# RWKV heads on their own row halves instead of a block-diagonal state, in a hybrid recurrent layer

## The chip, the cores and the metric

The kernel runs on one core of a Trainium2 chip. TensorE (PE) multiplies, VectorE (DVE), ScalarE (ACT) and GpSimd (POOL) do the elementwise work, and SyncE (SP), ACT and POOL issue the DMAs. The metric is the device time of one execution in microseconds (us); lower is better.

## The reference

One layer of a decoder trunk, for a prompt of 1024 tokens and for 8 single-token sequences that continue from given states:

```python
xn = _rmsnorm(x, norm1_g)
P  = xn @ w_in                       # one projection, its columns split among three groups
o_r, S_r = _rwkv7(...)               # 6 heads x 64: generalised delta rule
o_h, S_h = _hgrn2(...)               # 6 heads x 64: gated linear attention in chunks of 64
o_l, ... = _rglru(...)               # 256 channels: gated linear recurrence
x = x + concat(o_r, o_h, o_l) @ w_out
x = x + square(relu(_rmsnorm(x, norm2_g) @ w1)) @ w2      # 1024 -> 4096 -> 1024
y = _rmsnorm(x, final_g)
```

The change lies in the first group. For each head and token, with a 64x64 state S (value x key):

```python
sa = S @ (-kk_t)
S  = S * w_t + outer(sa, kk_t * a_t) + outer(v_t, k_t)
o  = S @ r_t
```

All arithmetic is fp32. Outputs are y for both groups and all final states.

## The kernel before

The kernel has two stages. In the first (to about 870 us) the input projection, the three recurrent groups and the output projection are woven together; in the second the MLP runs as dense matmuls. Dense products are three fp32r matmuls of 128x128 weights each (high and low parts), so the weights arrive twice: once through SP, once as an accumulating DMA that POOL issues (L267). Everything else on TensorE is plain fp32, where a matmul is two instructions in the trace.

**Order of the work.** Only TensorE's order is written by hand. `weave` (L82) is a planner: each piece of work is a generator that issues instructions and then yields either a delay in us or the name of an event it waits for. The planner keeps a clock `now`, which `mm` (L70) and `tr` (L75) advance by an estimated cost (0.08 for a 64x64x64 fp32 matmul, 0.11 for a transpose), and takes the stream that is ready; where none is, it issues dense matmuls of the projection as filler. Delays are the constants D1 to D42. The other engines' order follows from priorities. A late operand therefore stops TensorE and all that is queued behind it.

**RWKV.** Two heads share a tile of 128 channels, so there are 3 pairs j, and each half of the prompt (hf) is cut into two quarters of 256 tokens: 12 parts q (`PARTS`), each of NQ = 4 chunks of C = 64 tokens. Four generators work on each part:

- `rw_operands` (L490) makes decays and keys. It transposes v into `uv` (vT, L536 to L541: 2 transposes of 128x128, 2 ACT copies), writes the key operands `kb` (L544, L548) and `ar` (L549, L550), and transposes `kb` into `kbt` (L555 to L559: 4 transposes of 128x128, one ACT copy).
- `rw_inverse` (L573) runs as two streams, one for the even and one for the odd parts. It makes the scores `sc` (L583 to L592): for each head 4 matmuls of 64 rows by 128 columns, then a mask on DVE, with the delay D10 between the heads. Then it inverts unit triangular 64x64 blocks in five doublings (W and Y), and forms mv (L643).
- `rw_chain` (L651) goes through the chunks in order. For each: `ar` times the state (L667) and an add (rh, L669); ym times rh (L674) and a copy into uv (L675); then kbt times uv (L679), the output products with the state (L682) and with sc (L685), the decayed state on POOL (L690) and the new state (L696).
- `rw_finish` (L712) normalises, transposes the output back (oT, L730 to L732) and applies the gate.

The state of a pair is block-diagonal, 128x128, with zeros off the blocks; one matmul of 128 contracted rows serves both heads. A chunk's solved values lie on one half of the rows, by the parity of the chunk (`brow[c % 2]`), for both heads; `units` (L484) goes through the heads outside and the chunks inside.

**PSUM.** The banks have tags: `ra` (2 banks) for sc, W, Y and mv of both inverse streams, `ch` (1) for the chain, `o` (1) for the small products of operands, finish and the gated recurrence, `h` (2) and `big` (2) for the rest. A tile of a tag waits until the one that had its bank has been read.

Of the kernel before, what the change touches and what calls it, by code (L numbers as in the profile page):

```python
# [17 lines left out]
P = 128  # L18
D = 1024
# [31 lines left out]
def kernel(ctx: ExitStack, tc: tile.TileContext, i, o):  # L51
# [432 lines left out]
    def units():  # L484

        for h in range(2):
            for c in range(NQ):
                yield c, h, brow[c % 2], slice(((c // 2) * 2 + h) * C, ((c // 2) * 2 + h) * C + C)

    def rw_operands(q):  # L490
# [38 lines left out]
        kb = rwp.tile([P, NQ // 2, 4, C], F32, tag="kb", name=f"kb_{n}", bufs=1)  # L529
# [12 lines left out]
        ck4 = "p (c x t) -> p c x t"  # L542
        V.scalar_tensor_tensor(t5, t3, 1.0, t4, op0=ALU.add, op1=ALU.mult)
        V.scalar_tensor_tensor(kb[:, :, 1:3, :], t5.rearrange(ck4, x=2, t=C), 0.5, t1.rearrange(ck4, x=2, t=C),  # L544
                               op0=ALU.mult, op1=ALU.mult)
        V.tensor_scalar(t3, t3, hka[:, j:j + 1], omka[:, j:j + 1], op0=ALU.mult, op1=ALU.add)
        V.tensor_tensor(t3, t3, k_, op=ALU.mult)
        V.tensor_tensor(kb[:, :, 0:4:3, :], t3.rearrange(ck4, x=2, t=C), t1.rearrange(ck4, x=2, t=C), op=ALU.mult)  # L548
# [10 lines left out]
        S.copy(kbt, pt.rearrange("p (c x) -> p c x", x=P))  # L559
# [13 lines left out]
    def rw_inverse(q):  # L573
# [9 lines left out]
        for h in range(2):  # L583
            hp = slice(h * 64, h * 64 + 64)
            pt = ps("ra", f"sc{h}_{n}")
            for c in range(NQ):
                mm(pt[:, c * P:(c + 1) * P],
                   kb[hp, c // 2, 2 * (c % 2):2 * (c % 2) + 2, :].rearrange("p x t -> p (x t)"),
                   ar[hp, c, :, :].rearrange("p x t -> p (x t)"))
            V.tensor_tensor(sc.rearrange("p (c h) x -> p h c x", h=2)[:, h], pt.rearrange("p (c x) -> p c x", x=P),  # L590
                            bc(smask.rearrange("p x t -> p (x t)")[:, None, :], [P, NQ, P]), op=ALU.mult)
            if h == 0:  # L592
                yield D10
        ev(("sc", q), 0.0)
        sc5 = sc.rearrange("p (c e h) x -> p c e h x", e=2, h=2)
        for e in range(2):
            V.copy_predicated(ym[brow[e]].rearrange("p (c h) t -> p c h t", h=2),
                              bc(lmask[brow[e], 0, None, None, :].bitcast(I32), [64, NQ // 2, 2, 64]),
                              sc5[brow[e], :, e, :, 0:64])
# [44 lines left out]
        for c, h, b, cc in units():  # L644
            mm(pt[b, cc], sc[krow[c % 2], 2 * c + h, 0:64], uv[krow[c % 2], c, h * 64:h * 64 + 64])
# [5 lines left out]
    def rw_chain(q):  # L651
# [5 lines left out]
        pt = ps("ch", f"ch_{n}")  # L657
        po = pt[:, QT:2 * QT]
        for c in range(NQ):
            st = rw_state[j]  # L660
            b = brow[c % 2]
            first = st is None
            mv = xm[b, (c // 2) * 2:(c // 2) * 2 + 2, :].rearrange("p h v -> p (h v)")
            if first:
                rh = mv
            else:
                mm(pt[b, 0:P], ar[:, c, 0, :], st)  # L667
                rht = rwp.tile([P, P], F32, tag="rh", name=f"rh{c}_{n}", bufs=1)
                V.tensor_tensor(rht[b, :], pt[b, 0:P], mv, op=ALU.add)  # L669
                rh = rht[b, :]  # L670
# [4 lines left out]
            V.tensor_copy(uv[b, c, :], pt[b, 0:P])  # L675
# [12 lines left out]
            if not first:  # L688
                ws = rwp.tile([P, P], F32, tag="ws", name=f"ws{c}_{n}", bufs=2)
                G.tensor_scalar(ws, st, wc, 0.0, op0=ALU.mult, op1=ALU.add)  # L690
# [21 lines left out]
    def rw_finish(q):  # L712
# [18 lines left out]
        for c in range(NQ // 2):  # L731
            tr(pt[:, c * P:(c + 1) * P], ot[:, c * P:(c + 1) * P], ident)  # L732
# [818 lines left out]
```

## Time and profile before

| | us |
|---|---|
| three runs: median (lowest to highest) | 1645.81 (1644.93 to 1648.32) |
| profiled execution: device time | 1637.81 |
| its span, first to last instruction | 1636.0 |
| TensorE busy in the span | 1536.6 |
| VectorE / ScalarE / GpSimd busy | 759.2 / 650.0 / 386.2 |
| mean granted TensorE clock | 0.962 of full |

A row of the timeline gives the start in us from the span's beginning, the time that a group of like instructions took, engine, line, operation, "out<-moving,stationary", the weights' rows*columns and the moving tile, and the count. The start of the next row minus the start of this one is the time that the group held TensorE (its "slot"); the time in the row is longer, because a matmul's end overlaps its successors. L73 is the line of `mm`, L77 that of `tr`, so TensorE's work is told apart by tile names.

### The profile page before, as it was taken

The numbers are of one execution on the slowest core, as the hardware profiler recorded it, in microseconds if no ns is written. First come the engines' busy times: TensorE is split into PE (matmuls) and PEld (weight loads), VectorE is DVE, ScalarE is ACT, GpSimd is POOL, SyncE is SP. The second block draws the span as 40 slices with busy tenths as digits, with TensorE's granted clock in tenths as the row PEclk, the third lists the DMA queues.
The fourth block names the chain that finished last, engine by engine and source line by source line (L and its number), as shares of the span: only waits on it lengthen the run. The fifth ranks groups of instructions, "written<-read, shape, count | busy, mean of one in ns | idle before, by whom it ended". The sixth has DMA issues, their size and how long they took to land.

```text
span 1636.0 us, 29373 instructions
## 1 busy us (share of the span) xinstructions
PE 1536.6 (94%) x12158; PEld 1309.2 (80%) x12158; DVE 759.2 (46%) x1752; ACT 650.0 (40%) x1374; POOL 386.2 (24%) x505
## 2 busy tenths in 40 slices
PE   6879999999899999999868899999999999999997
PEld 5657677688688788777667798989898999898887
DVE  6486656775666676675434122222222222222224
ACT  4443643644345346355434323323242323333232
POOL 3472312322323424413222111111101010111111
PEclk8989989999799999999989899999999999999999
DMA  7624424333243433335564454444445453534342
GB/s 223 149 56 101 90 65 92 78 79 85 59 93 78 105 82 91 91 85 126 137 154 109 104 103 90 98 85 101 80 99 95 90 99 83 103 78 97 59 91 104
DMA packets 56373, 159.00 MB, mean 97 GB/s; under 512 B 7312, under 2 KB 7600, under 8 KB 56240
## 3 DMA queue, kind: packets, MB, share of 16 engines
q0 software_dynamic: 26288, 77.48, 28.3%
q1 hardware_dynamic: 29808, 79.61, 14.9%
q8 instruction: 95, 1.56, 0.4%
q14 instruction: 38, 0.31, 0.1%
q10 hardware_dynamic: 144, 0.04, 0.0%
HBM read 150.93 MB, written 6.17 MB: 96 GB/s over the span
## 4 chain that ended last, share of the span: by engine, by line
PE 73%; issue 8%; DVE 7%; DMA 6%; ACT 4%; POOL 3%; POOLq 0%; ACTq 0%; DVEq 0%
PE up L73 20%; PE dn L73 18%; PE in L73 16%; PE ch L73 3%; PE out L73 3%; DMA wl_in<-in_w_in 2%; DMA wl_w<-in_w 2%; PE W L73 2%; PE Y L73 2%; DMA wl_out<-in_w_out 2%; PE sc L73 1%; PE gram L73 1%; PE ho L73 1%; DVE rq L931 1%; POOL wl_w L267 1%
## 5 line engine op out<-in xcount | busy, mean ns | idle before, releaser
L73 PE MATMUL in<-xh,wl_in 128*128 128x512 f32 (+3 forms) x648 | 224.7, 347 | 12.7 <-DMA wl_in<-in_w_in 12.7
L73 PE MATMUL in<-xl,wh_in 128*128 128x512 f32 (+3 forms) x648 | 222.9, 344 | 4.5 <-DVE xl L356 4.5
L73 PE MATMUL dn<-hh,wl_w 128*128 128x264 f32 (+2 forms) x696 | 223.3, 321 | 0.6 <-DMA wl_w<-in_w 0.6
L73 PE MATMUL in<-xh,wh_in 128*128 128x512 f32 (+3 forms) x648 | 223.4, 345 | 0.0
L73 PE MATMUL dn<-hl,wh_w 128*128 128x264 f32 (+2 forms) x696 | 222.8, 320 | 0.0
L73 PE MATMUL dn<-hh,wh_w 128*128 128x264 f32 (+2 forms) x696 | 222.6, 320 | 0.0
L267 POOL DMA_DIRECT2D wl_w<-in_w x90 | 77.3, 865 | 590.2 <-ACT hh L1369 325.7
L1439 DVE TENSOR_TENSOR mix<-mix,dn 128x512 f32<-128x512 f32 (+2 forms) x192 | 98.3, 512 | 242.4 <-PE dn L73 242.4
L262 ACT ACTIVATE wh_w<-raw_w 128x512 fp32r<-128x512 f32 (+1 forms) x90 | 70.6, 785 | 275.1 <-PE dn L73 225.3
L1368 DVE SCALAR_TENSOR_TENSOR rl<-up,rl 128x512 f32<-128x512 f32 (+2 forms) x96 | 49.5, 516 | 219.1 <-ACT rl L1367 219.1
L73 PEld LDWEIGHTS in<-xh,wl_in 128*128 128x128 f32 x648 | 126.9, 196 | 29.4 <-DMA wl_in<-in_w_in 15.1
L73 PE MATMUL up<-nxh,wh_w 128*128 128x264 f32 (+1 forms) x512 | 144.9, 283 | 1.4 <-DVE rl L1368 1.3
L73 PE MATMUL up<-nxl,wh_w 128*128 128x264 f32 (+1 forms) x512 | 144.1, 281 | 0.5 <-POOL nxl L1267 0.5
L73 PE MATMUL up<-nxh,wl_w 128*128 128x264 f32 (+1 forms) x512 | 144.4, 282 | 0.0
L73 PEld LDWEIGHTS dn<-hh,wl_w 128*128 128x128 f32 x696 | 130.8, 188 | 14.3 <-DMA wl_w<-in_w 4.6
L73 PEld LDWEIGHTS in<-xl,wh_in 128*128 128x128 f32 x648 | 126.7, 195 | 17.9 <-DVE xl L356 4.8
L73 PEld LDWEIGHTS in<-xh,wh_in 128*128 128x128 f32 x648 | 126.8, 196 | 15.7 <-issue 4.7
L73 PEld LDWEIGHTS dn<-hl,wh_w 128*128 128x128 f32 x696 | 130.9, 188 | 10.1
L73 PEld LDWEIGHTS dn<-hh,wh_w 128*128 128x128 f32 x696 | 131.0, 188 | 9.4
L73 PE MATMUL up<-nh,wl_w 128*128 128x512 f32 x256 | 102.8, 402 | 8.4 <-DMA wl_w<-in_w 8.4
L1367 ACT ACTIVATE rl<-up 128x512 f32<-128x512 f32 (+2 forms) x96 | 43.3, 451 | 152.7 <-PE up L73 152.7
L73 PE MATMUL up<-nh,wh_w 128*128 128x512 f32 x256 | 102.5, 400 | 0.0
(436 smaller groups left out, 3228.6 us busy)
## 6 DMA issues: line engine op xcount, KB each, us to landing
raw_in<-in_w_in SPq DMA_DIRECT2D x53, 512.0 KB, 3.4
wl_in<-in_w_in POOLq DMA_DIRECT2D x52, 512.0 KB, 5.5
raw_w<-in_w SPq DMA_DIRECT2D x32, 512.0 KB, 3.3
wl_w<-in_w POOLq DMA_DIRECT2D x32, 512.0 KB, 5.5
raw_w<-in_w SPq DMA_DIRECT2D x64, 256.0 KB, 2.7
wl_w<-in_w POOLq DMA_DIRECT2D x58, 256.0 KB, 4.1
raw_out<-in_w_out SPq DMA_DIRECT2D x16, 512.0 KB, 3.4
wl_out<-in_w_out POOLq DMA_DIRECT2D x16, 512.0 KB, 5.5
```

Of the source, the lines that this page charges most:

```text
L73: PE.matmul(out, lhsT, rhs, start=start, stop=stop)
L262: act(wh[:, ks], raw[:, ks], AF.Copy)
L267: G.dma_start(wl[:, ks], src[:, ks], accum_op=ALU.add)
L931: V.tensor_tensor(rq[hp, h, :].rearrange("p (m j) -> p m j", j=hh), k4[hp, :, 1, :], q4[hp, :, 1, :], op=ALU.mult)
L1367: act(rl[:, :n], pt[:, :n], AF.Relu)
L1368: V.scalar_tensor_tensor(rl[:, :n], pt[:, :n], 0.0, rl[:, :n], op0=ALU.max, op1=ALU.mult)
L1439: V.tensor_tensor(x2[m][:, c0:c0 + n], x2[m][:, c0:c0 + n], pt[:, :n], op=ALU.add)
```

## The change

Head h of a pair is put on its own half of the rows throughout. The state becomes 128x64 and is no longer cleared at the start; products with it are two matmuls of 64x64 instead of one with 128 contracted rows. `units` goes through the chunks outside and the heads inside, so successive matmuls lie on alternating halves. vT and oT become 8 matmuls of 64x64 with an identity instead of 2 transposes of 128x128; kbt becomes 8 transposes of 64x128 in two groups with a delay D4 between them; kb holds three blocks per chunk, one of which ACT copies. The scores of both heads go to both `ra` banks at once, halves alternating, without the delay D10. In the chain uv is copied in two instructions instead of one and the state updated in one instead of two. The state written out is 128x64 instead of 128x128.

```diff
-    rw_st = [[rwp.tile([P, P], F32, name=f"st{j}_{q}") for q in range(2)] for j in range(3)]
-    for st in rw_st:
-        for q in range(2):
-            G.memset(st[q], 0.0)
-    brow = (slice(64, 128), slice(0, 64))
-    krow = (slice(0, 64), slice(64, 128))
+    rw_st = [[rwp.tile([P, C], F32, name=f"st{j}_{q}") for q in range(2)] for j in range(3)]
+
+    brow = (slice(0, 64), slice(64, 128))
+    krow = (slice(64, 128), slice(0, 64))
...
-        for h in range(2):
-            for c in range(NQ):
-                yield c, h, brow[c % 2], slice(((c // 2) * 2 + h) * C, ((c // 2) * 2 + h) * C + C)
+        for c in range(NQ):
+            for h in range(2):
+                yield c, h, brow[h], slice(c * C, c * C + C)
...
-        pt = ps("o", f"vT_{n}")
-        for c in range(NQ // 2):
-            tr(pt[:, c * P:(c + 1) * P], v[:, q0 + c * P:q0 + (c + 1) * P], ident)
-        pt4 = pt[:, 0:NQ // 2 * P].rearrange("p (c x) -> p c x", x=P)
-        S.copy(uv[0:64, 0:NQ:2, :], pt4[0:64])
-        S.copy(uv[64:128, 1:NQ:2, :], pt4[64:128])
+        pt = ps("o", f"vT_{n}")[:, 0:QT]
+        for c, h, b, cc in units():
+            mm(pt[krow[h], cc], v[b, q0 + c * C:q0 + c * C + C], ident[b, b])
+        for h in range(2):
+            S.copy(uv[krow[h], :, h * 64:h * 64 + 64], ck(pt[krow[h]]))
...
+        S.copy(kb[:, :, 2, :], kb[:, :, 0, :])
...
-        pt = ps("o", f"kbt_{n}")
-        for c in range(NQ):
-            src = kb[:, c // 2, 2 * (c % 2):2 * (c % 2) + 2, :].rearrange("p x t -> p (x t)")
-            tr(pt[:, c * P:(c + 1) * P], src, ident)
-        S.copy(kbt, pt.rearrange("p (c x) -> p c x", x=P))
+        for h in range(2):
+            b = brow[h]
+            pt = ps("o", f"kbt{h}_{n}")[:, 0:QT]
+            for c in range(NQ):
+                tr(pt[:, c * C:c * C + C], kb[b, c, h:h + 2, :].rearrange("p x t -> p (x t)"), ident[b, b])
+            S.copy(kbt[:, :, b], ck(pt))
+            if h == 0:
+                yield D4
...
-        for h in range(2):
-            hp = slice(h * 64, h * 64 + 64)
-            pt = ps("ra", f"sc{h}_{n}")
-            for c in range(NQ):
-                mm(pt[:, c * P:(c + 1) * P],
-                   kb[hp, c // 2, 2 * (c % 2):2 * (c % 2) + 2, :].rearrange("p x t -> p (x t)"),
-                   ar[hp, c, :, :].rearrange("p x t -> p (x t)"))
...
-            if h == 0:
-                yield D10
+        pts = [ps("ra", f"sc{h}_{n}") for h in range(2)]
+        for c, h, b, _ in units():
+            mm(pts[h][:, c * P:(c + 1) * P], kb[b, c, h:h + 2, :].rearrange("p x t -> p (x t)"),
+               ar[b, c, :, :].rearrange("p x t -> p (x t)"))
...
-                mm(pt[b, 0:P], ar[:, c, 0, :], st)
-                rht = rwp.tile([P, P], F32, tag="rh", name=f"rh{c}_{n}", bufs=1)
-                V.tensor_tensor(rht[b, :], pt[b, 0:P], mv, op=ALU.add)
+                for b in brow:
+                    mm(pa[b], ar[b, c, 0, :], st[b])
+                rht = rwp.tile([P, C], F32, tag="rh", name=f"rh{c}_{n}", bufs=1)
+                V.tensor_tensor(rht, pa, rh, op=ALU.add)
...
-            for h in range(2):
-                hc = slice(h * 64, h * 64 + 64)
-                mm(pt[b, hc], ym[b, (c // 2) * 2 + h, :], rh[:, hc])
-            V.tensor_copy(uv[b, c, :], pt[b, 0:P])
+            for b in brow:
+                mm(pu[b], ym[b, c, :], rh[b])
+            for b in brow:
+                V.tensor_copy(uv[b, c, b], pu[b])
             yield D17
-            for h in range(2):
-                hp = slice(h * 64, h * 64 + 64)
-                mm(pt[hp, P:P + 64], kbt[:, c, hp], uv[:, c, hp])
-            out = po[krow[c % 2], (c // 2) * P:(c // 2) * P + P]
+            for b in brow:
+                mm(pst[b], kbt[:, c, b], uv[:, c, b])
+            out = po[:, c * C:c * C + C]
             if not first:
-                mm(out, ar[:, c, 1, :], st, stop=False)
-            for h in range(2):
-                hp = slice(h * 64, h * 64 + 64)
-                mm(out[:, hp], sc[:, 2 * c + h, 64:128], uv[:, c, hp], start=first, stop=first or h == 1)
+                for b in brow:
+                    mm(out[b], ar[b, c, 1, :], st[b], stop=False)
+            for h, b in enumerate(brow):
+                mm(out[b], sc[:, 2 * c + h, 64:128], uv[:, c, b], start=first, stop=True)
...
-                    V.scalar_tensor_tensor(sn[hp, hp], pt[hp, P:P + 64], wc[hp], ws[hp, hp], op0=ALU.mult, op1=ALU.add)
+                V.scalar_tensor_tensor(sn, pst, wc, ws, op0=ALU.mult, op1=ALU.add)
...
-        for c in range(NQ // 2):
-            tr(pt[:, c * P:(c + 1) * P], ot[:, c * P:(c + 1) * P], ident)
+        for c, _, b, cc in units():
+            mm(pt[b, cc], ot[b, cc], ident[b, b])
```

More of the change, by code (lines that the diff above doesn't have):

```diff
@@ L528, in rw_operands @@
         ar = rwp.tile([P, NQ, 2, C], F32, tag="ar", name=f"ar_{n}", bufs=3)
-        kb = rwp.tile([P, NQ // 2, 4, C], F32, tag="kb", name=f"kb_{n}", bufs=1)
+        kb = rwp.tile([P, NQ, 3, C], F32, tag="kb", name=f"kb_{n}", bufs=1)
         kbt = rwp.tile([P, NQ, P], F32, tag="kbt", name=f"kbt_{n}", bufs=3)
@@ L582, in rw_inverse @@
         (S.copy if q < 2 else G.tensor_copy)(ym, bc(id64[:, None, :], [P, NQ, C]))
-        for h in range(2):
-            hp = slice(h * 64, h * 64 + 64)
-            pt = ps("ra", f"sc{h}_{n}")
-            for c in range(NQ):
-                mm(pt[:, c * P:(c + 1) * P],
-                   kb[hp, c // 2, 2 * (c % 2):2 * (c % 2) + 2, :].rearrange("p x t -> p (x t)"),
-                   ar[hp, c, :, :].rearrange("p x t -> p (x t)"))
-            V.tensor_tensor(sc.rearrange("p (c h) x -> p h c x", h=2)[:, h], pt.rearrange("p (c x) -> p c x", x=P),
+        pts = [ps("ra", f"sc{h}_{n}") for h in range(2)]
[3 more added lines that the diff above has]
+        for h, b in enumerate(brow):
+            sch = sc.rearrange("p (c h) x -> p h c x", h=2)[:, h]
+            V.tensor_tensor(sch, pts[h].rearrange("p (c x) -> p c x", x=P),
                             bc(smask.rearrange("p x t -> p (x t)")[:, None, :], [P, NQ, P]), op=ALU.mult)
-            if h == 0:
-                yield D10
+            V.copy_predicated(ym[b], bc(lmask[b, 0, None, :].bitcast(I32), [64, NQ, 64]), sch[b, :, 0:64])
         ev(("sc", q), 0.0)
[L595 to L599, printed above, removed]
         ymf, xmf = (t.rearrange("p u t -> p (u t)") for t in (ym, xm))
@@ L644, in rw_inverse @@
         for c, h, b, cc in units():
-            mm(pt[b, cc], sc[krow[c % 2], 2 * c + h, 0:64], uv[krow[c % 2], c, h * 64:h * 64 + 64])
+            mm(pt[b, cc], sc[krow[h], 2 * c + h, 0:64], uv[krow[h], c, h * 64:h * 64 + 64])
         S.copy(xmf, pt)
@@ L657, in rw_chain @@
         pt = ps("ch", f"ch_{n}")
+        pa, pu, pst = (pt[:, u * C:u * C + C] for u in range(3))
         po = pt[:, QT:2 * QT]
@@ L660, in rw_chain @@
             st = rw_state[j]
-            b = brow[c % 2]
             first = st is None
[L663 to L666, printed above, removed]
-                mm(pt[b, 0:P], ar[:, c, 0, :], st)
-                rht = rwp.tile([P, P], F32, tag="rh", name=f"rh{c}_{n}", bufs=1)
-                V.tensor_tensor(rht[b, :], pt[b, 0:P], mv, op=ALU.add)
-                rh = rht[b, :]
+            rh = xm[:, c, :]
@@ L671, in rw_chain @@
+            if not first:
+                for b in brow:
+                    mm(pa[b], ar[b, c, 0, :], st[b])
+                rht = rwp.tile([P, C], F32, tag="rh", name=f"rh{c}_{n}", bufs=1)
+                V.tensor_tensor(rht, pa, rh, op=ALU.add)
+                rh = rht
                 yield D16
-            for h in range(2):
-                hc = slice(h * 64, h * 64 + 64)
-                mm(pt[b, hc], ym[b, (c // 2) * 2 + h, :], rh[:, hc])
-            V.tensor_copy(uv[b, c, :], pt[b, 0:P])
+            for b in brow:
+                mm(pu[b], ym[b, c, :], rh[b])
@@ L683, in rw_chain @@
-            for h in range(2):
-                hp = slice(h * 64, h * 64 + 64)
-                mm(out[:, hp], sc[:, 2 * c + h, 64:128], uv[:, c, hp], start=first, stop=first or h == 1)
+                for b in brow:
+                    mm(out[b], ar[b, c, 1, :], st[b], stop=False)
+            for h, b in enumerate(brow):
+                mm(out[b], sc[:, 2 * c + h, 64:128], uv[:, c, b], start=first, stop=True)
             wc = ee[:, c, C:C + 1]
             sn = rw_st[j][c % 2]
-            if not first:
-                ws = rwp.tile([P, P], F32, tag="ws", name=f"ws{c}_{n}", bufs=2)
+            if first:
+                V.tensor_scalar(sn, pst, wc, None, op0=ALU.mult)
+            else:
+                ws = rwp.tile([P, C], F32, tag="ws", name=f"ws{c}_{n}", bufs=2)
@@ L690, in rw_chain @@
                 G.tensor_scalar(ws, st, wc, 0.0, op0=ALU.mult, op1=ALU.add)
-            for h in range(2):
-                hp = slice(h * 64, h * 64 + 64)
-                if first:
-                    V.tensor_scalar(sn[hp, hp], pt[hp, P:P + 64], wc[hp], None, op0=ALU.mult)
-                else:
-                    V.scalar_tensor_tensor(sn[hp, hp], pt[hp, P:P + 64], wc[hp], ws[hp, hp], op0=ALU.mult, op1=ALU.add)
+                V.scalar_tensor_tensor(sn, pst, wc, ws, op0=ALU.mult, op1=ALU.add)
@@ L1522, in outputs @@
     sh = r["shift"].transpose(2, 1, 0).reshape(1 + NB, D)
-    wkv = r["p_wkv"].reshape(3, 2, 64, 2, 64)
-    wkv = np.stack([wkv[:, h, :, h] for h in range(2)], axis=1).reshape(1, 1, 6, 64, 64)
+    wkv = r["p_wkv"].reshape(1, 1, 6, 64, 64)
     lru = r["lru"].reshape(256, 36)
```

8 lines of the change are left out of this document (3 added, 5 removed).

## Prediction

> **What bounds the kernel now.** I read the page first, then the busy time by windows, then TensorE's waits, then its timeline around the operations that the change touches.
>
> ```profile
> span 1636.0 us, 29373 instructions
> ## 1 busy us (share of the span) xinstructions
> PE 1536.6 (94%) x12158; PEld 1309.2 (80%) x12158; DVE 759.2 (46%) x1752; ACT 650.0 (40%) x1374; POOL 386.2 (24%) x505
> ```
> ```profile
> 50.00:800.00 750.00, 705.81 (x6935) 562.43 (x6933) 484.07 (x1192) 356.90 (x863) 247.64 (x316) 0.95 0.40 91
> 800.00:870.00 70.00, 50.06 (x359) 48.83 (x360) 22.73 (x47) 24.26 (x38) 16.82 (x20) 0.85 0.54 129
> ```
> ```profile
> PE oT L77 <- DVE ot L727: 15.0, 7, 5.2
> PE out L73 <- DMA wl_out<-in_w_out: 12.5, 4, 10.4
> PE pb_kk L77 <- DVE t L247: 11.2, 4, 8.9
> PE ch L73 <- DVE rh L669: 3.3, 5, 1.7
> ```
>
> The columns of the windows are start and end, length, then busy us of PE, weight loads, DVE, ACT and POOL, the granted clock, DMA share and GB/s. All of RWKV lies in these two windows. In the 750 us from 50 to 800 TensorE is busy 706, DVE 484, ACT 357, POOL 248: TensorE is the bound, in an order that is fixed, with dense matmuls put into the gaps. It idles 44 us there. The waits that are named (times, longest last) are the output's transpose behind the normalisation, a transpose of the key norm and weights for the output projection; the chain's own wait, ch on rh, is 3.3 us. So the chain's latency is mostly covered, and what counts is how long each piece of the change holds TensorE. That is not its busy time but its slot, from its start to the next start.
>
> **The unit prices**, from the timeline at full clock.
>
> ```profile
> 759.26 0.40 PE L73 MATMUL out<-mh,wh_out 128*128 128x512 f32 x1
> 759.50 0.40 PE L73 MATMUL out<-ml,wh_out 128*128 128x512 f32 x1
> 759.83 0.43 PE L73 MATMUL ch<-st,ar 128*64 128x128 f32 x2
> 760.19 0.50 PE L73 MATMUL out<-mh,wl_out 128*128 128x512 f32 x1
> ```
> ```profile
> 762.23 0.44 PE L73 MATMUL ch<-rh,ym 64*64 64x64 f32 x4
> 762.61 0.65 PE L77 MATMUL hoT<-ident,hot 128*128 128x128 f32 x4
> 763.02 0.47 PE L73 MATMUL out<-ml,wh_out 128*128 128x512 f32 x1
> ```
> ```profile
> 764.57 0.34 PE L73 MATMUL ch<-uv,kbt 128*64 128x64 f32 x4
> 764.74 0.38 PE L73 MATMUL ch<-st,ar 128*64 128x128 f32 x2
> 764.96 0.40 PE L73 MATMUL ch<-uv,sc 128*64 128x64 f32 x4
> 765.28 0.44 PE L77 MATMUL oT<-ident,ot 128*128 128x128 f32 x2
> 765.48 0.48 PE L73 MATMUL out<-ml,wh_out 128*128 128x512 f32 x1
> ```
> ```profile
> 578.14 0.68 PE L73 MATMUL Y<-ym,wm 64*64 64x64 f32 x16
> 578.75 0.39 PE L73 MATMUL in<-xl,wh_in 128*128 128x264 f32 x1
> ```
>
> First, a change of tile shape costs 0.09 us each way: a dense matmul holds TensorE 759.50 - 759.26 = 0.24 before another dense one, but 0.33 before ch, whose weights are 128*64. Second, four instructions (two fp32 matmuls) on the same half take 762.61 - 762.23 = 0.38 with the change of shape behind them; the four of kbt, whose outputs alternate between the column halves, take 764.74 - 764.57 = 0.17 without one, so about 0.26 with one. Third, 16 alternating instructions take 578.75 - 578.14 = 0.61, one change included.
>
> **The change part by part**, in slots. There are 12 parts of 4 chunks; 45 of the 48 chunks have a state before them.
>
> ```profile
> L669 DVE TENSOR_TENSOR rh<-ch,xm 64x128 f32<-64x128 f32 x45 | 12.9, 286 | 15.3 <-PE ch L73 12.7 <-ACT wm L620 1.5 <-ACT hf L854 0.3
> L675 DVE COPY uv<-ch 64x128 f32<-64x128 f32 x48 | 13.7, 286 | 14.2 <-PE ch L73 13.3
> L696 DVE SCALAR_TENSOR_TENSOR st<-ch,ee,ws 64x64 f32<-64x64 f32 x90 | 25.4, 282 | 26.0 <-PE ch L73 25.0
> ```
>
> *Chain.* `ar` times the state is one matmul now, 760.19 - 759.83 = 0.36; it becomes two alternating ones of 64x64, 0.26: -0.10 x45 = -4.5. `ym` times rh, 0.38, becomes 0.26: -0.12 x48 = -5.8. The third step is one run of 128*64 shapes, 765.28 - 764.57 = 0.71. After the change the state product in its middle is 64*64 between two of 128*64, so the run has two more changes of shape: 3 x 0.26 = 0.78, and that is +0.07 x45 = +3.2. Together -7.1.
>
> On DVE a chunk has four instructions before (one rh, one uv, two st) and four after (one, two, one), and the rows give 0.29 for 64x128 and 0.28 for 64x64: width is not what costs, so DVE is level. The second uv copy delays the third step by 0.29; in the chunk shown `ym` is through at 762.23 + 0.44 = 762.67 and kbt starts at 764.57, so 1.9 us of dense work covers two copies (0.57). Without that cover it would cost 0.29 x48 = 14 us, but the single state update gives 0.28 back in the same loop.
>
> *Scores.*
>
> ```profile
> 586.65 0.28 PE L73 MATMUL in<-xh,wh_in 128*128 128x272 f32 x1
> 586.77 0.29 PE L73 MATMUL in<-xl,wh_in 128*128 128x272 f32 x1
> 586.99 1.16 PE L73 MATMUL sc<-ar,kb 64*128 64x128 f32 x8
> 588.08 0.40 PE L73 MATMUL in<-xh,wl_in 128*128 128x272 f32 x1
> ```
> ```profile
> 299.68 0.69 PE L73 MATMUL hS<-vt,kt 64*64 64x64 f32 x32
> ```
>
> A head's group holds TensorE 588.08 - 586.99 = 1.09, and entering it costs 0.22 - 0.12 = 0.10; two groups are 2.38 a part. Afterwards one group of 16 alternates the row halves, each into a bank of its own. If the halves overlap fully it is 1.19: -1.19 x12 = -14.3. If not at all, eight more instructions of (1.09 - 0.10) / 8 = 0.12 make it 2.18: -0.20 x12 = -2.4. The trace has no 128-column weights on alternating halves. The nearest row is hS, 32 instructions over all four quarters of the array in 0.69, which at the 0.38 per four of one half would be about 3. I take full overlap.
>
> The Trainium skill ("TensorE: Matmul & The Clock Gate", section "Packing small matmuls — row/col tiling") gives 3.07 times for four row tiles, 77% of full; for two halves that would be 1.54 times, an estimate of 2.18 / 1.54 = 1.42 a part, a saving of 11.5 in place of 14.3, and the sum 2.8 higher. No run here shows it yet.
>
> *Transposes.* Before, vT and oT are two transposes of 128x128, in the dense shape: 765.48 - 765.28 = 0.20. Each becomes eight alternating 64x64 matmuls, like the Y row, entered from another shape: 0.61 + 0.09 = 0.70. That is +0.50 x24 = +12.0. Where a neighbour has the 64*64 shape already, both changes of shape go: +0.32 x24 = +7.7 is the low end.
>
> kbt is four transposes, as hoT 763.02 - 762.61 = 0.41. It becomes two groups of four on one half, 64 moving columns each.
>
> ```profile
> 579.10 0.95 PE L73 MATMUL hqk<-bones,qk 128*128 128x2 f32 x8
> 579.91 0.68 PE L73 MATMUL gate<-pm_xg,gup 128*128 128x256 f32 x2
> ```
> ```profile
> L73 PEld LDWEIGHTS bonus<-t,bones x24: 186/188/333, 83.1 to 696.8; 128*128 128x128 f32 x24
> L77 PEld LDWEIGHTS kbt<-ident,kb x48: 138/140/230, 80.6 to 680.8; 128*128 128x128 f32 x48
> ```
>
> By moving columns a group is like `ym`'s, 0.38 + 0.09 = 0.47, two are 0.94: +0.53 x12 = +6.4. By weights it is dearer: hqk moves 2 columns, and still takes 0.81 / 8 = 0.10 an instruction for its 128 columns of weights; then a group is 0.41 + 2 x 0.09 = 0.59, and the sum +0.77 x12 = +9.2. I take the first, since a transpose's weight load takes 140 ns where a matmul's takes 188.
>
> The Trainium skill (the same page, section "LDWEIGHTS (loading the stationary operand)") has the load go by columns, never by rows, about 107 ns for 128; by that rule halving the rows saves nothing, kbt stands at the dear end, and the sum is 2.8 higher. hqk's row agrees, for matmuls.
>
> *Sum of slots:* -7.1 - 14.3 + 12.0 + 6.4 = **-3.0 us**.
>
> *What else moves.*
>
> ```profile
> 585.69 0.68 PE L73 MATMUL Y<-ym,wm 64*64 64x64 f32 x16
> ```
> ```profile
> 586.95 0.34 DVE L635 COPY_PREDICATED ym<-cmask,Y 128x128 f32<-128x128 int32 x1
> ```
> ```profile
> L590 DVE TENSOR_TENSOR sc<-sc,cmask 128x512 f32<-128x512 f32 x24 | 16.5, 689 | 11.6 <-PE sc L73 11.4
> L620 ACT COPY wm<-W x48: 346/372/430, 114.2 to 734.9; 128x256 f32<-128x256 f32 x48
> L559 ACT COPY kbt<-kbt x12: 570/586/632, 81.5 to 681.2; 128x512 f32<-128x512 f32 x12
> ```
>
> The scores now need both `ra` banks at once. In the part shown the other inverse stream's Y has one, and DVE reads it until 586.95 + 0.34 = 587.29, while the scores start at 586.99: TensorE, with all that is queued behind, would stand 0.30. I take half of the parts for such (an estimate; the two streams run half a part apart): +1.8. ACT gets two copies of 0.37 for one of 0.59 and one more of about 0.37 for kb's third block, 0.5 a part, at 357 of 750 us. The third block has the 6.4 us of D7 to be ready; the second kbt group has D4, 1.6 us, for the first one's copy in the single `o` bank. Both are covered unless ACT is 1.2 us behind. POOL has half the columns in L690 and loses the clearing of the states at the start, where I count nothing. D4 added and D10 dropped are equal, so the last part, which the output projection waits for, comes out level.
>
> The planner charges the new transposes 1.28 us a part more (16 x 0.08 + 8 x 0.11 against 8 x 0.11), close to the 1.53 that they cost, and knows nothing of the overlap. So dense cover stays about where it was.
>
> **Total:** -3.0 + 1.8 = -1.2 us, on a span of 1636.0. The profiled execution took 1637.81, 8.0 below the median of the three runs, so I carry the difference over to the median: 1645.81 - 1.2 = 1644.6, no change. About 0.2% (3.3 us) is what a measurement can tell.
>
> **Rivals.**
>
> 1. *The scores' halves don't overlap* (128 columns of weights for each half share one path). For it: no row shows the case. Against: hS. Then -2.4 stands for -14.3: 1656.5, slower.
> 2. *The banks take the place of the delay.* Both `ra` banks are held from the first score to the masks, 0.69 each on DVE, and the other stream's W or Y stands before TensorE. For it: two streams on two banks, DVE at 484 of 750. Against: W, Y and sc are not among TensorE's long waits now. Standing 0.30 before and 0.69 after in each part is 12 x 1.0 = 12 against the 1.8 counted: 1654.8, slower. It decides from 0.5 us a part, where 6 us outweigh the -3.0 by 3.
> 3. *Neighbours share the shape, and waits shrink.* vT and oT at their low end give -4.3, no bank is waited for (-1.8), and with the inverse starting 1.6 + 1.19 us sooner a quarter of the 18.3 us that oT and ch wait now goes (-4.6): 1633.9, faster. For it: much 64*64 work lies around. Against: oT waits for the normalisation, which keeps its place.
> 4. *Two matmuls are too few to alternate.* Then steps one and two stay at 0.38 and step three is 0.26 + 0.38 + 0.38 = 1.02, +0.31: 45 x (0.02 + 0.31) = +14.9 for -7.1, 1666.6. The kbt row (two matmuls, 0.17) speaks against it.
>
> **How the numbers follow.** My forecast, no change, has 0.38 (own range 1637 to 1653, from the low end of vT and oT to the dear kbt with half of the scores' gain lost); the rivals 0.17, 0.17, 0.24 and 0.04. Within 0.2%: 0.22 from the forecast and 0.11 from the milder ends of rivals 1 to 3. Faster: 0.10 and 0.21 from rival 3. Slower: 0.06, 0.26 from rivals 1 and 2, 0.04 from rival 4. The range of 8 in 10 reaches from rival 3 to rivals 1 and 2: 1633 to 1659.
>
> **What would show it.** In the changed kernel's timeline at full clock: scores x16 in one slot of about 1.1 (2.2 by rival 1); chain slots 0.26, 0.26 and 0.78; vT and oT about 0.6 before the next start; two kbt groups with 0.38 each (0.50 if weights set it). In TensorE's waits: sc, W or Y with more than 5 us speak for rival 2; oT well under 15 us for rival 3. A difference of over 10 us with these slots as forecast would prove the reasoning wrong: then latency, or the order on the other engines, is the bound, and not slots.

## Result and profile after

The changed kernel is slower: 1646.63 us median (1640.84 to 1658.29, 20 runs) against 1636.45 (1627.57 to 1649.28, 20 runs) for the kernel before on the same chip, a ratio of 1.0061 (95% interval 1.0038 to 1.0085), about 10 us. The 1645.81 of the three runs shown beforehand was at the upper end of that scatter. All comparisons below are such ratios; 0.001 is 1.6 us.

The profiled execution of the changed kernel took 1644.92 us. Its page and its windows, with the same columns as before:

```profile
span 1643.1 us, 30510 instructions
...
PE 1526.1 (93%) x12722; PEld 1298.9 (79%) x12722; DVE 745.3 (45%) x1752; ACT 657.4 (40%) x1398; POOL 382.5 (23%) x499
```
```profile
50.00:800.00 750.00, 690.36 (x7445) 546.74 (x7444) 467.35 (x1186) 358.56 (x874) 243.28 (x316) 0.95 0.40 89
800.00:870.00 70.00, 50.47 (x386) 48.42 (x385) 27.78 (x55) 30.08 (x52) 17.88 (x20) 0.92 0.62 147
```

These lines already divide the result. TensorE is busy 1526.1 us instead of 1536.6, so 10.5 less: the change did take work away. But it stands idle 1643.1 - 1526.1 = 117.0 us instead of 1636.0 - 1536.6 = 99.4, so 17.6 more. The difference of the two is the 7.1 us by which the span grew. Nearly all of the added idle time lies between 50 and 800 us, where idle time went from 750 - 705.8 = 44.2 to 750 - 690.4 = 59.6. The granted clock is the same (0.961 and 0.962). ScalarE has 7 us more to do, VectorE 14 less, and neither is near its limit.

TensorE's waits after, in the stretch of RWKV (us, times, longest):

```profile
PE pb_kk L77 <- DVE t L247: 16.1, 3, 12.7
PE oT L73 <- DVE ot L714: 9.4, 3, 6.3
...
PE pw L73 <- ACT lgq L1125: 4.3, 1, 4.3
PE ch L73 <- DVE uv L666: 3.9, 4, 1.4
PE pw L73 <- ACT lxb L1125: 3.9, 1, 3.9
PE ch L73 <- DVE rh L660: 2.5, 1, 2.5
PE pw L73 <- DVE bo L565: 2.3, 1, 2.3
```

The three rows of pw, 10.5 us, were not there before; pw is a product of the next part's operands, and what it waits for here is the reader of the `o` bank's last tile. pb_kk has grown from 11.2 to 16.1; oT has fallen from 15.0 to 9.4. The chain (ch) has grown from 3.5 to 6.4: its wait for uv, which is copied in two instructions now, from 0.2 to 3.9. W and Y wait 1.6 in all, mv not at all. So of what the change rewrote it is chiefly the chain that waits longer, by 2.9 us; most of the new waiting is in work that was not rewritten and now comes at another time.

The pieces themselves, from the timeline at full clock:

```profile
763.43 0.33 PE L73 MATMUL ch<-rh,ym 64*64 64x64 f32 x4
763.69 0.50 PE L73 MATMUL out<-ml,wh_out 128*128 128x512 f32 x1
...
764.81 0.68 PE L73 MATMUL oT<-ident,ot 64*64 64x64 f32 x16
765.42 0.34 PE L73 MATMUL ch<-uv,kbt 128*64 128x64 f32 x4
765.69 0.33 PE L73 MATMUL ch<-st,ar 64*64 64x64 f32 x4
765.95 0.34 PE L73 MATMUL ch<-uv,sc 128*64 128x64 f32 x4
766.21 0.50 PE L73 MATMUL out<-mh,wl_out 128*128 128x512 f32 x1
```
```profile
588.41 1.16 PE L73 MATMUL sc<-ar,kb 64*128 64x128 f32 x16
589.50 0.69 PE L73 MATMUL gram<-rq,kq 128*64 128x64 f32 x16
```
```profile
576.57 0.46 PE L77 MATMUL kbt<-ident,kb 64*128 64x64 f32 x4
576.96 0.39 PE L73 MATMUL s_mean<-s_os,bones 128*128 128x8 f32 x2
```

ym times rh holds TensorE 763.69 - 763.43 = 0.26, the third step 766.21 - 765.42 = 0.79, oT 0.61, the scores of both heads 1.09 in one group of 16, a kbt group 0.39. The page told that busy time fell; these rows tell that at full clock the pieces cost about what they were priced at.

### The profile page after: what moved, and what is told of

Read it like the earlier page. It is cut to its first block, busy times and chain, and to the rows that moved or that the text cites. A ratio compares the mean times of both kernels' runs of the same rounds, so it can differ in the third digit from the quotient of the medians.

```text
span 1643.1 us, 30510 instructions
## 1 busy us (share of the span) xinstructions
PE 1526.1 (93%) x12722; PEld 1298.9 (79%) x12722; DVE 745.3 (45%) x1752; ACT 657.4 (40%) x1398; POOL 382.5 (23%) x499
## 3 DMA queue, kind: packets, MB, share of 16 engines
q0 software_dynamic: 26288, 77.39, 28.3%
## 5 line engine op out<-in xcount | busy, mean ns | idle before, releaser
L73 PE MATMUL in<-xh,wl_in 128*128 128x512 f32 (+3 forms) x648 | 223.0, 344 | 16.9 <-DMA wl_in<-in_w_in 16.9
L73 PE MATMUL in<-xl,wh_in 128*128 128x512 f32 (+3 forms) x648 | 224.9, 347 | 0.3 <-DVE xl L356 0.3
L73 PE MATMUL dn<-hh,wl_w 128*128 128x264 f32 (+2 forms) x696 | 223.2, 321 | 1.3 <-DMA wl_w<-in_w 1.3
L73 PE MATMUL in<-xh,wh_in 128*128 128x512 f32 (+3 forms) x648 | 224.4, 346 | 0.0
L73 PE MATMUL dn<-hh,wh_w 128*128 128x264 f32 (+2 forms) x696 | 223.1, 320 | 0.0
L73 PE MATMUL dn<-hl,wh_w 128*128 128x264 f32 (+2 forms) x696 | 222.9, 320 | 0.0
L73 PEld LDWEIGHTS in<-xh,wl_in 128*128 128x128 f32 x648 | 127.3, 196 | 30.1 <-DMA wl_in<-in_w_in 18.6
L73 PE MATMUL up<-nxh,wh_w 128*128 128x264 f32 (+1 forms) x512 | 145.8, 285 | 1.4 <-DVE rl L1355 1.3
L73 PE MATMUL up<-nxl,wh_w 128*128 128x264 f32 (+1 forms) x512 | 145.0, 283 | 0.5 <-POOL nxl L1254 0.5
L73 PE MATMUL up<-nxh,wl_w 128*128 128x264 f32 (+1 forms) x512 | 145.2, 284 | 0.0
L73 PEld LDWEIGHTS dn<-hh,wl_w 128*128 128x128 f32 x696 | 131.0, 188 | 14.8 <-DMA wl_w<-in_w 4.9
L73 PEld LDWEIGHTS in<-xl,wh_in 128*128 128x128 f32 x648 | 127.3, 197 | 15.3 <-issue 2.1
L73 PEld LDWEIGHTS dn<-hl,wh_w 128*128 128x128 f32 x696 | 131.1, 188 | 10.1
L73 PEld LDWEIGHTS dn<-hh,wh_w 128*128 128x128 f32 x696 | 131.2, 188 | 9.4
L73 PEld LDWEIGHTS in<-xh,wh_in 128*128 128x128 f32 x648 | 127.4, 197 | 14.1 <-issue 2.4
L73 PE MATMUL up<-nh,wl_w 128*128 128x512 f32 x256 | 102.8, 402 | 8.8 <-DMA wl_w<-in_w 8.8
L73 PE MATMUL up<-nh,wh_w 128*128 128x512 f32 x256 | 102.6, 401 | 0.0
```

The source lines that it names most:

```text
L73: PE.matmul(out, lhsT, rhs, start=start, stop=stop)
```

## Experiments

The table lists the two kernels and eighteen variants, with the span, busy and idle time and mean granted clock of the profiled execution; then each variant follows with its edit. The profiled execution is not always near the median: f1's was its slowest run (1645.04 us, median 1638.16), g1's its fastest (1626.24, median 1637.97). The ratios are of medians over all runs.

| kernel | ratio to before (95%) | span | TensorE busy | idle | clock |
|---|---|---|---|---|---|
| before | 1 | 1636.0 | 1536.6 | 99.4 | 0.962 |
| changed | 1.0061 (1.0038 to 1.0085) | 1643.1 | 1526.1 | 117.0 | 0.961 |
| e1, h bank | 1.0037 (1.0007 to 1.0067) | 1641.0 | 1515.9 | 125.1 | 0.965 |
| e2, scores by head | 1.0139 (1.0098 to 1.0179) | 1658.0 | 1547.6 | 110.4 | 0.957 |
| e3, before, scores alternating | 1.0030 (1.0002 to 1.0058) | 1640.3 | 1520.7 | 119.6 | 0.960 |
| n1, before, charges and D4 | 1.0095 (1.0063 to 1.0127) | 1647.8 | 1536.4 | 111.4 | 0.962 |
| n3, before, charges | 1.0135 (1.0101 to 1.0170) | 1663.1 | 1540.8 | 122.3 | 0.956 |
| n4, before, charges less | 1.0007 (0.9984 to 1.0030) | 1638.9 | 1537.6 | 101.3 | 0.963 |
| f1, D10 | 1.0002 (0.9975 to 1.0029) | 1643.3 | 1530.0 | 113.3 | 0.955 |
| f2, h bank, D10 | 0.9925 (0.9893 to 0.9956) | 1620.7 | 1511.2 | 109.5 | 0.969 |
| f3, old charges, D10 | 1.0013 (0.9988 to 1.0038) | 1638.0 | 1524.9 | 113.1 | 0.961 |
| f4, old charges | 1.0143 (1.0102 to 1.0185) | 1663.2 | 1535.2 | 128.0 | 0.955 |
| e6, old charges, h bank | 1.0128 (1.0095 to 1.0160) | 1661.2 | 1532.2 | 129.0 | 0.952 |
| e5, old charges, h bank, D10 | 0.9883 (0.9853 to 0.9913) | 1617.7 | 1508.8 | 108.9 | 0.968 |
| g1, e6 with the delay before W | 0.9983 (0.9956 to 1.0010) | 1624.5 | 1511.2 | 113.3 | 0.968 |
| g2, e5 without that delay | 1.0163 (1.0133 to 1.0192) | 1662.3 | 1536.4 | 125.9 | 0.950 |
| g3, e3 with D10 | 0.9932 (0.9907 to 0.9956) | 1626.0 | 1511.8 | 114.2 | 0.966 |
| g4, e5, state product last | 0.9849 (0.9825 to 0.9872) | 1612.8 | 1503.6 | 109.2 | 0.966 |
| h1, before without D10 | 1.0008 (0.9980 to 1.0037) | 1637.4 | 1531.6 | 105.8 | 0.960 |
| h2, g4 with more delay | 0.9926 (0.9899 to 0.9954) | 1629.7 | 1508.9 | 120.8 | 0.964 |

The theory to begin with was that the cost lies in the plan: the planner is charged 1.28 us a part more, and the second kbt group stands behind D4 and the `o` bank, so that other work meets late operands. The rivals were the scores (no overlap, or the two `ra` banks) and the new work itself (a second uv copy, two kbt copies, kb's third block).

**e1, the second kbt group in an `h` bank, without D4.**

```diff
-            pt = ps("o", f"kbt{h}_{n}")[:, 0:QT]
+            pt = ps("h" if h else "o", f"kbt{h}_{n}")[:, 0:QT]
-            if h == 0:
-                yield D4
```

> The changed kernel, but the second group of kbt transposes goes to a bank of tag h and follows the first at once, without the delay D4. Theory 1 (the second turn in the single o bank and its delay make the operands late, and TensorE then waits for pw and pb_kk): most of the loss goes, 6 to 10 us below the changed kernel, ratio to before about 1.001, and the pw and pb_kk waits, 26 us together in the changed kernel, fall under 15. Theory 2 (the slots of the new small matmuls are dearer than I counted): no difference to the changed kernel, ratio 1.006. Theory 3 (any shift of the planner's order moves the time by some us either way): a change of up to 8 us without its waits being those of pw and pb_kk.

1.0037. The waits of pw went down to 0.9 us, another came: pb_kk for a step of the gated recurrence (lcar), 13.5 us in one piece. The gain is 4 us where the theory gave 6 to 10, and the interval overlaps that of the changed kernel, so by itself the second turn in the bank is at most a small part.

**e2, the scores head by head again, with D10, in the changed kernel.**

```diff
-        for c, h, b, _ in units():
-            mm(pts[h][:, c * P:(c + 1) * P], ...)
+        for h, b in enumerate(brow):
+            pt = ps("ra", f"sc{h}_{n}")
+            for c in range(NQ):
+                mm(pt[:, c * P:(c + 1) * P], ...)
...
+            if h == 0:
+                yield D10
```

> The changed kernel, but the scores by head again, four matmuls on one half, a mask, D10, then the other half. If the alternating halves overlap and slots count: 12 us are lost, ratio to before about 1.013. If holding both ra banks costs as much as the overlap gains: no difference to the changed kernel, 1.006. If the banks are what made the change slower: 5 us or more better, under 1.003.

1.0139: 13 us slower than the changed kernel, and 22 us slower than the changed kernel with D10 (f1, below), from which it differs in the scores alone. So the overlap is real and worth at least what the slots say, and the `ra` banks do not cost as much as it gains.

**e3, the kernel before with alternating scores into both banks, without D10.** The edit is the one of e2 turned round.

> The kernel before, with nothing changed but the scores: both banks at once, halves alternating, no D10. If slots count, the gain of 14 us that I put down for the scores stands alone: ratio 0.991 to 0.994. If latency or order decides and freed slots turn into waits: 0.998 to 1.002. If the two ra banks are the trouble: above 1.003.

1.0030, on the border between the second and the third expectation. TensorE is busy 15.9 us less than before (1520.7 for 1536.6) and idle 20.2 more. This is the changed kernel's pattern, with none of its other parts: freed slots turn into waits. The waits of pb_kk went from 11.2 to 28.3 us, those of sc, W, Y and mv together from 2.2 to 7.7; so the two `ra` banks have a part in it, but the smaller one.

```profile
PE pb_kk L77 <- DVE t L247: 26.6, 7, 18.0
```

**n1, n3, n4, the kernel before with the planner's clock moved, no work changed.** n1:

```diff
             tr(pt[:, c * P:(c + 1) * P], v[:, q0 + c * P:q0 + (c + 1) * P], ident)
+        now[0] += 0.42
...
         S.copy(kbt, pt.rearrange("p (c x) -> p c x", x=P))
+        now[0] += 0.44
+        yield D4
...
             tr(pt[:, c * P:(c + 1) * P], ot[:, c * P:(c + 1) * P], ident)
+        now[0] += 0.42
```

n3 is n1 without the D4, n4 is n3 with minus signs.

> The kernel before with the same work, but the planner's clock is charged 1.28 us a part more (0.42 after vT, 0.44 after kbt, 0.42 after oT) and waits D4 after kbt, so that the order of the dense matmuls between the steps moves as in the changed kernel. Theory 3 (order alone): ratio 1.003 to 1.007, though no work was added. Theories 1 and 2: 0.998 to 1.002.

> The kernel before with the planner's clock advanced by 0.42 more at vT, 0.44 at kbt and 0.42 at oT, without the D4 that the other one had; the work is the same. If the charges shift the order and that costs, about 1.005 to 1.010, with waits of pw or pb_kk grown. If D4 was what cost in that kernel, 0.998 to 1.002.

> The kernel before with the planner's clock set back by 0.42 at vT, 0.44 at kbt and 0.42 at oT, the opposite sign. If too high a charge means that too little dense cover is placed, too low a charge places more and is level or better: 0.996 to 1.000. If the order of before is a tuned point from which any shift of the clock loses, it is slower too: 1.004 to 1.010.

1.0095, 1.0135 and 1.0007. The charges alone cost 22 us in the kernel before, with the same instructions, and 16 with the D4; both are more than was expected. The opposite sign costs nothing. So far this spoke for the charges as the cause in the changed kernel.

**The three parts of the plan in the changed kernel, in all combinations** (e1 above is one, the changed kernel another). "Old charges" sets the clock back behind the new transposes; "D10" puts the delay back behind the first head's mask:

```diff
+        now[0] -= 0.42
         for h in range(2):
             S.copy(uv[krow[h], :, h * 64:h * 64 + 64], ck(pt[krow[h]]))
...
+        now[0] -= 0.44
         if q >= 2:
...
             V.copy_predicated(ym[b], ...)
+            if h == 0:
+                yield D10
...
             mm(pt[b, cc], ot[b, cc], ident[b, b])
+        now[0] -= 0.42
```

> The changed kernel with the planner's clock as before the change: after the new transposes the clock is set back by what they charge more (0.42 for vT, 0.44 for kbt, 0.42 for oT), the second kbt group goes to an h bank at once instead of waiting D4 for the o bank, and the delay D10 stands again, behind the first head's mask. So the planner sees the costs and delays of before, with the new instructions. Order theory: the 10 us come from the planner's charges and delays, so they go, and of the 11 us by which the slots fell a part shows: ratio to before 0.993 to 1.000. Rival (the price is in the new work itself: second uv copy, two kbt copies, ACT's third block): the ratio stays at 1.004 to 1.008. The waits pw on lgq and pb_kk on t are back near 0 and 9 by the order theory.

> As the kernel with the old plan, but without the delay D10, so the scores of both heads go out at once and the inverse starts sooner, as in the changed kernel. If only charges and D4 cost, as the order theory has it, it is like that kernel or up to 2 us better: 0.992 to 1.000. If the missing D10 is what disturbs the order (the kernel of before with alternating scores lost its gain in waits), it is 3 to 6 us above it: 1.000 to 1.004. Rival (price in the work itself): 1.004 to 1.008.

> The changed kernel with the delay D10 alone put back behind the first head's mask. Three parts of the plan are in question: charges, D4 or the h bank for the second kbt group, D10. So far: changed kernel 1.006, h bank 1.004, h bank and old charges 1.013, all three 0.988. D10 theory: without the delay the inverse's first steps come before DVE is through the masks, so D10 is worth some 20 us wherever it stands: 0.990 to 0.997. Plan theory: no part has a price of its own, any change of the plan shifts which work meets which, by up to 1% either way: 0.995 to 1.012, no pattern over the eight combinations.

> The changed kernel with D10 and the h bank, charges as changed. D10 theory: 0.985 to 0.994, below the 1.004 of the h bank alone by over 10 us. Plan theory: anywhere from 0.990 to 1.012; if the charges are what matters once D10 stands, near 1.000, since only the kernel with all three was fast.

> The changed kernel with D10 and the old charges, the second kbt group still in the o bank behind D4. D10 theory: 0.986 to 0.996. If the o bank's second turn is what costs (a late pw, which waits for that bank), it is 5 us or more above the fast kernel, at 0.992 to 1.000, with waits of pw that the fast kernel has not. Plan theory: 0.990 to 1.012.

> The changed kernel with the old charges alone, D4 and no D10 as changed. D10 theory: no gain without D10, 1.004 to 1.013. Charge theory (what the planner is charged for the new transposes is what costs, as in the kernel before, where charging them without the work gave 1.010 and 1.013): 0.995 to 1.000. Plan theory: 0.995 to 1.012.

| | `o` bank, D4 | `o` bank, D4, D10 | h bank | h bank, D10 |
|---|---|---|---|---|
| charges as changed | 1.0061 | 1.0002 | 1.0037 | 0.9925 |
| old charges | 1.0143 | 1.0013 | 1.0128 | 0.9883 |

The ranges did badly: e5 came out better than any of its theories, e6 worse than all three, f1 and f3 above the range of the D10 theory and f4 just above it, and only f2 inside. What can be read is the pattern of signs. The charge theory fell: without D10 the old charges make it slower (by 0.008 and 0.009), with it they are worth +0.001 and -0.004. D10 is the one part with the same sign in all four pairs: -0.0059, -0.0112, -0.0130, -0.0245, or 10 to 40 us, and in each pair the two intervals lie apart. Put back alone it removes the whole loss of the changed kernel (1.0002), but brings no gain. The h bank without D4 is lower in all four pairs, clearly (-0.008 and -0.013) only where D10 stands; how much of that is the bank and how much the D4, no run tells. With old charges, D10 and the h bank the new layout is 1.2% faster than the kernel before.

The pair at the bottom right has old charges and the h bank, without D10 and with it: pages, then waits of the chain and of oT.

```profile
PE 1532.2 (92%) x12722; PEld 1307.2 (79%) x12722; DVE 748.2 (45%) x1752; ACT 656.0 (39%) x1398; POOL 382.2 (23%) x499
```
```profile
PE 1508.8 (93%) x12722; PEld 1287.6 (80%) x12722; DVE 748.3 (46%) x1752; ACT 655.4 (41%) x1398; POOL 380.6 (24%) x499
```
```profile
PE oT L73 <- DVE ot L714: 7.2, 2, 4.3
...
PE ch L73 <- DVE uv L666: 3.8, 4, 1.7
...
PE ch L73 <- DVE rh L660: 1.5, 3, 0.6
```
```profile
PE oT L73 <- DVE ot L716: 1.9, 2, 1.0
...
PE ch L73 <- DVE rh L662: 1.6, 1, 1.6
...
PE ch L73 <- DVE uv L668: 0.2, 1, 0.2
```

The same 12722 TensorE instructions take 23.4 us less busy time, because the clock is 0.968 for 0.952 (1508.8 x 0.968 and 1532.2 x 0.952 are both about 1460), and 20.1 us less idle time. Of the idle time some 10 us are the chain and oT, which wait mostly for VectorE. They fall in all four pairs (all rows of ch and oT together, including small ones: 17.0 to 7.9, 21.6 to 4.9, 10.4 to 6.1, 13.3 to 3.7). But they are not the account of the loss: the kernel before has 18.5 us of them, more than the changed one. Whether the inverse as a whole runs ahead can be looked for in the products mv, which end an inverse; the rows give their count, durations, and first and last start, before and after the change:

```profile
L73 PE MATMUL mv<-uv,sc x192: 218/218/366, 148.5 to 755.3; 64*64 64x64 f32 x192
```
```profile
L73 PE MATMUL mv<-uv,sc x192: 217/218/268, 151.9 to 743.8; 64*64 64x64 f32 x192
```

The last inverse starts its mv 11.5 us sooner, in a kernel that ends 7 us later. This is not D10 alone: with D10 put back the last start moves from 743.8 to 760.0 (f1), but with the h bank from 751.1 to 728.7 (f2) and in the pair above from 758.6 to 744.9 (e5). So the lead of the last inverse does not tell the slow kernels from the fast.

**g1 and g2, which side of D10 it is.** D10 delays the first W of the inverse, and it also parts the two masks on VectorE and releases the next part's operands later. g1 is e6 with only the first, g2 is e5 with only the second:

```diff
-        yield D11
+        yield D11 + D10
```
```diff
-        yield D11
+        yield D11 - D10
```

> The changed kernel with old charges and h bank (1.013 without D10, 0.988 with it), without D10 between the masks but with D10 added to D11, the delay between the masks and the first W. So the inverse's matmuls start as late as in the fast kernel, while both masks stand in one row on VectorE and the next part's operands are released 1.6 us sooner. If the later start of the inverse is what D10 is good for: 0.986 to 0.994. If it is the gap between the masks or the release of the operands: 1.006 to 1.014.

> The fast kernel (old charges, h bank, D10, 0.988) with D10 taken off D11: the masks have their gap and the operands of the next part are released late, but the inverse's matmuls start as soon as without D10. If the later start of the inverse is what counts: 1.006 to 1.014. If the gap or the release counts: 0.986 to 0.994. Values between mean that both do.

0.9983 (from e6's 1.0128) and 1.0163 (from e5's 0.9883). The later start of the inverse's matmuls in the plan is needed: without it the gap between the masks does nothing. With it the gap and the later release add another 0.010. Both came out just above their ranges, so both parts count, the delay first. The waits of the chain and oT do not tell these two apart (10.4 us in g1, 8.7 in g2); those of W and Y do, 5.9 against 11.2, and most of g2's is Y behind the masks:

```profile
PE Y L73 <- DVE sc L588: 8.6, 6, 2.5
```

**g3 and h1, D10 in the kernel before**, with alternating scores (e3 and D10) and as it was (D10 removed).

> The kernel before with alternating scores (1.003) and the delay D10 put back behind the first head's mask. D10 theory: the scores' 12 to 14 us of slots now show, 0.989 to 0.996. If the freed time of the scores can't become gain in this order at all, whatever the delay: 0.999 to 1.005.

> The kernel before without the delay D10 between the two heads' scores, all else as it was. If the dropped delay costs by itself, whatever the layout: 1.006 to 1.016. If it costs only together with scores that overlap (16 in 1.2 us where the planner counts 3.4): 0.998 to 1.003.

g3 gives 0.9932: with D10 the freed slots of the scores, 16 us off e3, show in the time. h1 gives 1.0008: with the scores by head D10 can go for nothing. So it is not the delay by itself, but the delay together with scores that overlap. g3 also shows what the new layout is not needed for: 11 us come from the order of the scores alone, nearly as much as the whole layout has in f2 (0.9925).

**g4 and h2, further from e5.** g4 puts the output's product with the state behind the ones with sc, so that kbt and sc, both 128*64, stand together:

```diff
-            if not first:
-                for b in brow:
-                    mm(out[b], ar[b, c, 1, :], st[b], stop=False)
             for h, b in enumerate(brow):
-                mm(out[b], sc[:, 2 * c + h, 64:128], uv[:, c, b], start=first, stop=True)
+                mm(out[b], sc[:, 2 * c + h, 64:128], uv[:, c, b], stop=first)
+            if not first:
+                for b in brow:
+                    mm(out[b], ar[b, c, 1, :], st[b], start=False)
```

> The fast kernel (0.988) with the third step's output products in another order: those with sc first, those with the state last, so that kbt and sc (128*64) stand together and the third step has one change of shape fewer: 0.09 x 45 = 4 us of slots. If slots become gain in an order without long waits: 0.984 to 0.987. If the state's product then waits for nothing but the bank and the order is as before, no change: 0.987 to 0.990.

0.9849, with this third step in its timeline:

```profile
704.10 0.34 PE L73 MATMUL ch<-uv,kbt 128*64 128x64 f32 x4
704.27 0.29 PE L73 MATMUL ch<-uv,sc 128*64 128x64 f32 x4
704.49 0.33 PE L73 MATMUL ch<-st,ar 64*64 64x64 f32 x4
704.75 0.50 PE L73 MATMUL out<-mh,wl_out 128*128 128x512 f32 x1
```

The step holds TensorE 0.65 instead of 0.79: 0.14 x 45 = 6.3 us. The span fell 4.9 us and the ratio 0.0034 (5.6 us), with idle time unchanged (109.2 for 108.9) and busy time 5.2 us less. The two ratios' intervals overlap, so it is the traces that speak here: where the waits stay as they are, slots do become time. g4, at 0.9849, is the fastest kernel found, 1.5% below the kernel before.

h2 is g4 with `yield D11 + D10`, 1.6 us more delay.

> The fastest kernel (0.985) with another 1.6 us of delay before the first W. If the inverse still starts too early (its W comes 9 to 10 us after the last mask there, its operands long ready, so a later start harms nothing by itself): 0.978 to 0.984. If the delay has a tuned place: 0.986 to 0.995.

0.9926: slower than g4 by 13 us, with 11.6 us more idle. The delay has a tuned place; more is not better.

## Why the prediction was wrong

- **The slot prices held at full clock, the sum was too high.** Scores 1.09 in one group (1.1 given), chain 0.26 and 0.79 (0.26 and 0.78), oT 0.61, kbt 0.39 a group (0.38). Added up over all rows from 50 to 870 us, start to next start without the named idle time, the chain went from 69.9 to 60.6 (-9.3, forecast -7.1), the scores from 28.8 to 16.3 (-12.5, forecast -13.1), kbt from 6.0 to 9.4 (+3.4, forecast +4.2), vT and oT from 8.2 to 15.6 (+7.4, forecast +9.8). The forecasts are given here without the change of shape on entering a group, since that stands in the row ahead of it. Together -11.0, where these forecasts add up to -6.2 and with the entries to the -3.0 of the sum; TensorE as a whole was busy 10.5 us less. The transposes were sized too low before the change: on average vT and oT cost 8.2 / 24 = 0.34 each, not 0.20, and kbt 6.0 / 12 = 0.50 a part, not 0.41. This error went the way of a gain and is not why the kernel is slower.
- **Rivals 1, 2 and 4 did not happen in the changed kernel.** The scores overlap fully, the rows of sc, W, Y and mv wait 1.6 us in all (rival 2 needed more than 5), and two matmuls do alternate. But rival 2's wait comes back with D10: in f1 the rows of Y are 8.4 us, 6.4 of them behind the masks (`PE Y L73 <- DVE sc L588: 6.4, 3, 2.3`).
- **The step that failed** is in the part on what else moves: "D4 added and D10 dropped are equal", and "dense cover stays about where it was" because the planner's charges were close to the costs. Two delays of 1.6 us were set off against each other by their size. But D4 stands in the operands and D10 stood ahead of the inverse. With scores that overlap, the loss of D10 costs 10 us in the changed kernel (f1) and 16 in the kernel before (e3 to g3). The same part put the second kbt group in the `o` bank behind D4 at nothing ("Both are covered"); once D10 stands, that costs another 13 us (f1 to f2). With both put right, f2 is 12 us faster than the kernel before, close to the 11 us of slots; without them the two losses outweigh the slots, which fits the measured +10.
- **Rival 3 had the sign of this wrong.** It took an inverse that starts 1.6 + 1.19 us sooner as a reason for less waiting. oT's wait did shrink (15.0 to 9.4), but pw, pb_kk and the chain took more than that, and e6 against g1 and g2 against e5 show that starting the inverse sooner in the plan costs 24 and 46 us.
- **The test that was named did its work.** A difference of over 10 us with the slots as forecast was said to mean that latency, or the order on other engines, is the bound. From the forecast of -1.2 to the measured +10 is such a difference, and delays and one bank, with no matmul changed, move it from a loss to a gain: the order was the bound. It was TensorE's own planned order, though, rather than that of the other engines.
- **The page of the Trainium skill** ("TensorE: Matmul & The Clock Gate", section "Packing small matmuls — row/col tiling") would have put 16 overlapping scores, with the entry of the group, at an estimated 1.42; the row has 1.09, or 1.19 with the 0.10 for entering, and 1.09 is what one head's eight instructions held before, so two row halves overlapped wholly. By the section "LDWEIGHTS (loading the stationary operand)" kbt would have stood at its dear end; the group of 0.39 with a change of shape in it, (0.39 - 0.09) / 4 = 0.075 a transpose, is below the 107 ns that it gives for 128 columns. Neither rule would have told the sign.

What stays open: why the overlap makes D10 matter, and by which waits it costs. The planner counts 3.41 us for the 16 scores (16 x 128/600); they held TensorE 2.38 by head and 1.19 now, with the entries, so between the scores and the first W less real time passes for the same planned delay, and D10 would make up for it. That fits h1, e3, g3 and h2, but no run changed that charge alone. n1, n3 and h2 also show that moving the plan by 1 to 3 us a part can cost 13 to 22 us with no score changed, so that D10's price is shown by the pairs that differ in it and not by a mechanism. Nor is it settled which early meeting of streams starts the longer waits; the old charges help with D10 and the h bank and harm without D10, which no theory here foresaw.

## What to carry to other kernels

In a kernel whose TensorE order is written by a planner with tuned delays, a sum of slots tells what a change can give, not what it does: before pricing a dropped or added delay at its size, ask which stream starts sooner for it, and who then reaches operands that are not ready. When work falls and idle time grows by more, put the old delays and charges back one at a time and together before giving up the change: here the same layout ran from 1.014 to 0.988 by the plan alone. And split a change into its parts in the old kernel as well: 11 us came from the order of the scores alone.

## What the runs showed of the hardware

Waits cost twice. In the windows below the granted clock falls to half within a wait and stays there for 13.7 and 17.1 us, four and five times 3.4. They are windows of the changed kernel around the 12.7 us wait of pb_kk and a pw wait of 3.88; the rows of these and of another pw wait come first (the bracket holds the wait and what ended it):

```profile
93.78 0.51 PE L73 MATMUL pw<-pm_wa,waup 64*128 64x256 f32 x1 [4.28 <-ACT lgq L1125]
...
114.17 0.66 PE L77 MATMUL pb_kk<-ident,t 128*128 128x128 f32 x2 [12.68 <-DVE t L247]
...
208.19 1.22 PE L73 MATMUL pw<-pm_wa,waup 64*128 64x256 f32 x2 [3.88 <-ACT lxb L1125]
```
```profile
101.50:104.30 2.80, 0.00 (x0) 0.00 (x0) 2.77 (x6) 0.18 (x1) 2.80 (x4) 1.00 0.10 41
104.30:118.00 13.70, 3.83 (x10) 2.81 (x10) 9.94 (x15) 3.96 (x5) 11.11 (x17) 0.50 0.26 42
118.00:131.70 13.70, 13.70 (x127) 10.30 (x126) 5.88 (x13) 7.16 (x12) 1.08 (x2) 1.00 0.39 90
```
```profile
206.70:223.80 17.10, 14.84 (x59) 9.27 (x60) 8.39 (x20) 6.75 (x14) 3.30 (x4) 0.50 0.16 29
```

The clock (third column from the end) is half from 2.8 us into the wait of pb_kk to 3.8 us after it. The Trainium skill ("TensorE: Matmul & The Clock Gate", section "What's actually happening") has half rate after an idle window of about 3.4 us and full rate after a busy one. The return to full rate agrees; the fall came somewhat sooner than a whole idle window, here and in the last row (2.4 us into the wait of 3.88). The last row also differs at its end: TensorE is busy 14.84 of 17.10 us and stays at half all the time. In the kernel before, from 196.6 to 220.4 us, it is busy 23.04 of 23.80 us and at half. Over the kernels here the mean clock was 0.950 to 0.969; between g2 and g1, with the same matmuls, idle time differs by 12.6 us and busy time, by the clock, by another 25.2.

A change of tile shape was dear where many small products meet: removing one from the third step saved 0.14 of 0.79 us, more than the 0.09 that was read from dense neighbours.
